# GpSimd subtractions for T2 and T4 of the weights' differences in a decoder layer's gate and up projections

## The chip, the cores and the metric

The kernel runs on one core of one Trainium2 chip. The metric is the device time of one execution in microseconds; the time before is the median of three runs. The profile is of one execution of its own.

## What is computed

The reference is one layer of a decoder (16 meta tokens ahead of 512 positions, width 1024): sparse attention, a layer norm, a SwiGLU feed-forward of width 2816, a second layer norm. The change lies in the feed-forward's first half:

```
def swiglu(h, w_gate, w_up, w_down):
    return (jax.nn.silu(h @ w_gate) * (h @ w_up)) @ w_down

ffn = swiglu(h, ffn_w_gate[i], ffn_w_up[i], ffn_w_down[i])
h = layer_norm(DEEPNORM_ALPHA * h + ffn, ln2_g[i], ln2_b[i])
```

## The kernel before

Every matmul works on a value split in two (a rounded high part, which ScalarE copies, and the rest, which a subtraction gives), so that three products of parts (high·high, high·low, low·high) stand for one fp32 product. Engines run in the order in which the program lists their instructions.

The gate and up projections go through 22 blocks f of 128 features of each. A block's weights are a 2 by 2 matrix of pieces, each 128 partitions by 512 columns: c0 = gate, first half of the depth; c1 = up, first half; c2 = up, second half; c3 = gate, second half. They lie side by side in `wgu[f]`. Blocks 1 to 21 use the Strassen-Winograd scheme: seven products of 12 matmuls instead of eight. Four of them take differences of weights:

- T1 = c1 − c0 (the program's product number 5), T3 = c2 − c1 (number 7),
- T2 = c2 − T1 (number 6), T4 = c3 − T2 (number 4).

Numbers 1, 2 and 3 take c0, c3 and c2 as they are. From block 3 on the products run in the order (f,5), (f,6), (f,2), (f,7), (f+1,1), (f,3), (f,4); `order` holds the list of all of them, and step n of the loop at the end of `trunk` issues product n.

Before product n a step does, in this order: `after` evaluates product n−1 (VectorE adds it to others: m after 6, v and uu after 7, uu after 3, sg and hid after 4; ScalarE's silu after 2 and 4; VectorE's m must have read the bank before product 7 adds to it, and uu before product 3 does); `prepare` splits the weights of the product four steps on (`right_part`: ScalarE writes the high part w, VectorE the low part w); `begin` starts the loads and the differences of later blocks, by distances in steps from (f,5), which `base[f]` holds:

```
LEAD = 4
LOAD_X, SUM_A, LOAD_Y, SUM_B, SUM_C = 20, 13, 11, 7, 3
```

`load_x` and `load_y` load c0,c1 (tile r_x, "upper") and c2,c3 (tile ry, "lower") by SyncE's queue. `sums_a` makes T1 and T3 at once: ScalarE writes −(c0,c1) into a wide tile T (128 by 1024), and a DMA on GpSimd's queue reads c1,c2 from memory and adds them to it (`plus`, line 899). `sums_b` makes T2: ScalarE writes −T1 into a third piece of the wide tile, and an accumulating DMA adds c2. `sums_c` makes T4 the same way from T2, in a tile of its own, with c3. There are two wide tiles, so that T of block f+2 takes the place of block f's. GpSimd does nothing else in this stage from block 3 on.

Of the kernel before, what the change touches and what calls it, by code (L numbers as in the profile page):

```python
# [14 lines left out]
ALU = mybir.AluOpType  # L15
# [58 lines left out]


LEAD = 4
LOAD_X, SUM_A, LOAD_Y, SUM_B, SUM_C = 20, 13, 11, 7, 3
TAIL = 4


# [40 lines left out]
def trunk(ctx, tc, a, out):  # L121
    nc = tc.nc
# [8 lines left out]
    def unit(name, dt=F32, tag="u"):  # L131
        return up.tile([P, UNIT], dt, name=name, tag=tag, bufs=UNITS[tag])
# [25 lines left out]
    def act_copy(o, i, scale=1.0):  # L158
        nc.scalar.activation(o, i, AF.Copy, scale=scale)  # L159
# [680 lines left out]
    upper, lower = {}, {}  # L840
# [54 lines left out]
    right, tsum = {}, {}  # L895

    def plus(o, f, c0, c1):

        nc.gpsimd.dma_start(o, a["wgu"][f][:, c0:c1], accum_op=ALU.add)  # L899
# [7 lines left out]

    def sums_b(f):

        act_copy(tsum[f, 6], tsum[f, 5], scale=-1.0)  # L910
        plus(tsum[f, 6], f, 1024, 1536)

    def sums_c(f):

        tsum[f, 4] = unit(f"T4{f}", tag="kq")[:, :512]
        act_copy(tsum[f, 4], tsum[f, 6], scale=-1.0)
        plus(tsum[f, 4], f, 1536, 2048)

    def begin(n):

        for f in range(2, NF):
            if n == base[f] - LOAD_X and f > 2:
                load_x(f)
            if n == base[f] - LOAD_Y:
                load_y(f)

            if f > 2 and n == max(base[f] - SUM_A, order.index((f - 2, 7)) - LEAD + 2):
                sums_a(f)
            if n == base[f] - SUM_B:
                sums_b(f)  # L930
            if n == base[f] - SUM_C:
                sums_c(f)
# [292 lines left out]
    for b in range(NB):  # L1225
        if b:
            po[1, b] = bank(f"po1{b}", "mm")
        if b == 1:
            normed(0)
            sums_a(1)  # L1230
        if b == 2:

            nc.scalar.activation(small("silu", 1, bufs=6), half_neg, AF.Silu)
        if b == 3:
            sums_b(1)
            prepare(6)
        for k in range(0 if b else 6, KT):
            out_terms(1, k, b)
            if b > 1 and k == LATE:
                turn_norm(b - 2)  # L1240
                normed(b - 1)
        residual(1, b)
        norm(b)
    for n, x in enumerate(order):
        if n == 1:
            sums_a(2)
            normed(3)
        if n == 3:
            turn_norm(2)
            sums_c(1)  # L1250
        if n:
            after(*order[n - 1])
        if n == 5:
            turn_norm(3)
            left_sum(5)
        prepare(min(n + LEAD, len(order)))
        begin(n)
        if n in (7, 9, 12):
            left_sum({7: 6, 9: 7, 12: 3}[n])
        product(*x)  # L1260
        if n == len(order) - 8:
            load(g_ff, 0)
            load(g_ff, 1)
        if n == len(order) - 4:
            hidden_parts(4)
        if n == len(order) - 2:
            cut(g_ff, 0)
# [134 lines left out]
```

## Time and profile before

| | |
|---|---|
| median of 3 runs | 679.12 us (678.54 to 680.46) |
| the profiled execution's own time | 681.46 us |
| its span, first to last instruction | 679.7 us |
| TensorE busy, share of the span | 654.9 us, 96% |
| VectorE / ScalarE / GpSimd busy | 507.9 / 390.5 / 243.2 us |
| DMA queue of GpSimd (q0) | 22.55 MB, 19.8% of 16 engines' span |

The stages along the span: projections and attention up to about 313 us, gate and up projections from 313 to 550 us, the down projection and the last norm to the end. PE stands for TensorE's matmuls, PEld for its weight loads, DVE for VectorE, ACT for ScalarE, POOL for GpSimd. A tile's name (T, w, ry) covers all its buffers; so T in a row can be T1, T2, T3 or T4. L159 and L162 are the helpers `act_copy` and `sub`, L1177 the helper `add` of `after`, so that only tiles tell what such a row is.

### The profile page before, as it was taken

The page shows a single profiled execution, that of the slowest core. Times are in us where ns is not written, and L with a number is a line of the kernel's source. Part 1 is how long each engine was busy: PE and PEld are TensorE (multiplying, and loading weights), DVE is VectorE, ACT ScalarE, POOL GpSimd, SP SyncE. Part 2 cuts the span into 40 slices and gives each one's busy share as a digit, 9 for nine tenths or more (in the row PEclk, how much of TensorE's full clock was granted, in tenths as well). Part 3 has the DMA queues.
Part 4 walks back from the last instruction along what each step waited for, and adds up shares of the span by engine and source line. Part 5 has one row for each costly group of instructions (what it writes and reads, how often), then busy time and mean ns, then how long its engine had stood idle before and what let it go on. Part 6 is the DMA issues. An engine that isn't in the chain of part 4 may idle for free.

```text
span 679.7 us, 11626 instructions
## 1 busy us (share of the span) xinstructions
PE 654.9 (96%) x4196; PEld 588.7 (87%) x4196; DVE 507.9 (75%) x1064; ACT 390.5 (57%) x775; POOL 243.2 (36%) x286
## 2 busy tenths in 40 slices
PE   8999999999999999999899999999999999999995
PEld 6888787888998897889799999899999988888884
DVE  5589898888987888777876767667676676687536
ACT  5573512467777675736766767657666556535420
POOL 2063812497776676556222223222222100011003
PEclk9999999999999999999999999999999999999998
DMA  6547130542242336535688998898997757755611
GB/s 237 174 146 261 60 76 7 148 151 76 71 118 71 111 79 213 158 102 132 138 187 193 205 223 177 199 204 190 225 199 158 203 185 241 234 168 192 203 47 62
DMA packets 41177, 105.80 MB, mean 156 GB/s; under 512 B 4784, under 2 KB 9952, under 8 KB 41120
## 3 DMA queue, kind: packets, MB, share of 16 engines
q1 hardware_dynamic: 31328, 82.12, 37.6%
q0 software_dynamic: 9360, 22.55, 19.8%
q8 instruction: 33, 0.54, 0.3%
q10 hardware_dynamic: 432, 0.39, 0.2%
q14 instruction: 24, 0.20, 0.1%
HBM read 96.88 MB, written 5.27 MB: 150 GB/s over the span
## 4 chain that ended last, share of the span: by engine, by line
PE 38%; issue 33%; DMA 12%; DVE 7%; ACT 5%; POOL 4%; SPq 0%; DVEq 0%; POOLq 0%; ACTq 0%
DMA T<-in_wgu 11%; PE po L773 6%; PE av L728 3%; POOL T L899 3%; PE pv L290 2%; PE pv L288 2%; PE pv L289 2%; PE pt L698 2%; ACT T L159 2%; PE p_q L290 2%; PE p_q L289 2%; PE p_q L288 2%; PE p_k L288 1%; PE p_k L290 1%; PE p_k L289 1%
## 5 line engine op out<-in xcount | busy, mean ns | idle before, releaser
L899 POOL DMA_DIRECT2D T<-in_wgu x63 | 54.7, 869 | 163.2 <-ACT T L159 152.9
L1319 PE MATMUL pd<-h_wd,hp 128*128 128x512 f32 (+1 forms) x324 | 91.1, 366 | 0.0
L162 DVE TENSOR_TENSOR w<-T,w 128x512 fp32r<-128x512 f32 x84 | 57.7, 688 | 24.7 <-ACT w L159 24.0
L1152 PE MATMUL pb<-s,w 128*128 128x256 f32 x504 | 68.2, 285 | 4.5 <-DVE m L1177 2.9
L1152 PE MATMUL pd<-s,w 128*128 128x256 f32 x504 | 67.4, 284 | 2.4 <-DVE uu L1177 1.7
L1152 PE MATMUL pa<-s,w 128*128 128x256 f32 x504 | 67.5, 284 | 1.8 <-ACT m L159 1.8
L1152 PEld LDWEIGHTS pb<-s,w 128*128 128x128 f32 x504 | 63.4, 192 | 6.1 <-ACT T L159 3.8
L1319 PEld LDWEIGHTS pd<-h_wd,hp 128*128 128x128 f32 x324 | 58.6, 189 | 10.1
L1152 PEld LDWEIGHTS pd<-s,w 128*128 128x128 f32 x504 | 63.2, 192 | 3.4 <-ACT T L159 2.3
L1152 PEld LDWEIGHTS pa<-s,w 128*128 128x128 f32 x504 | 63.5, 192 | 2.0 <-ACT m L159 2.0
L162 DVE TENSOR_TENSOR l_wd<-r_wd,h_wd 128x1024 fp32r<-128x1024 f32 x36 | 44.0, 1224 | 28.1 <-ACT h_wd L159 27.9
L672 POOL TENSOR_TENSOR lg<-lg,rec 128x144 f32<-128x144 f32 (+1 forms) x64 | 52.5, 844 | 22.7 <-DVE rec L670 21.9
L1319 PE MATMUL pd<-l_wd,hp 128*128 128x512 f32 (+1 forms) x162 | 59.7, 368 | 0.1
L159 ACT ACTIVATE h_wd<-r_wd 128x1024 fp32r<-128x1024 f32 x36 | 38.0, 1058 | 34.2 <-PE pd L1319 17.7
L159 ACT ACTIVATE w<-T 128x512 fp32r<-128x512 f32 x84 | 50.4, 621 | 5.8 <-DMA T<-in_wgu 5.6
L646 POOL TENSOR_TENSOR bm<-score,tz 128x256 f32<-128x256 f32 (+1 forms) x64 | 43.7, 714 | 16.0 <-DVE mn L655 15.5
L1040 POOL TENSOR_TENSOR fr<-fr,half_neg 128x1 f32<-128x1 f32 x4 | 4.0, 1006 | 121.8 <-DVE fr L1039 121.3
L663 ACT ACTIVATE lg<-lg,mn 128x272 f32<-128x272 f32 (+1 forms) x64 | 36.3, 570 | 11.6 <-DVE mn L655 11.6
L288 PE MATMUL p_k<-hTh,h_wk 128*128 128x264 f32 x128 | 37.8, 295 | 2.3 <-DVE q L331 2.3
L159 ACT ACTIVATE T<-T 128x512 f32<-128x512 f32 x42 | 26.4, 630 | 18.3 <-DMA T<-in_wgu 18.1
L290 PE MATMUL p_k<-hTh,l_wk 128*128 128x264 f32 x128 | 36.5, 285 | 0.0
L289 PE MATMUL p_k<-hTl,h_wk 128*128 128x264 f32 x128 | 36.4, 284 | 0.0
(360 smaller groups left out, 1739.4 us busy)
## 6 DMA issues: line engine op xcount, KB each, us to landing
r_wd<-in_wd SPq DMA_DIRECT2D x36, 512.0 KB, 4.2
r_x<-in_wgu SPq DMA_DIRECT2D x22, 512.0 KB, 8.7
T<-in_wgu POOLq DMA_DIRECT2D x21, 512.0 KB, 7.7
T<-in_wgu POOLq DMA_DIRECT2D x42, 256.0 KB, 5.3
ry<-in_wgu SPq DMA_DIRECT2D x20, 512.0 KB, 6.9
kb<-ka SPq DMA_DIRECT2D x32, 132.0 KB, 2.3
r_wq<-in_wq SPq DMA_DIRECT2D x8, 512.0 KB, 4.5
r_wk<-in_wk SPq DMA_DIRECT2D x8, 512.0 KB, 3.4
```

The source lines that it names most:

```text
L159: nc.scalar.activation(o, i, AF.Copy, scale=scale)
L162: eng.tensor_tensor(out=o, in0=x, in1=y.bitcast(F32), op=ALU.subtract)
L288: nc.tensor.matmul(o, lh, rh, start=i == 0, stop=False)
L289: nc.tensor.matmul(o, lh, rl, start=False, stop=False)
L290: nc.tensor.matmul(o, ll, rh, start=False, stop=i == KT - 1)
L646: nc.gpsimd.tensor_tensor(out=bm.at(b, W[b] - n, W[b]), in0=mask.at(b, W[b] - n, W[b]), in1=tzs[h][:, 256 - n :], op=ALU.add)
L663: nc.scalar.activation(lg.blk(b), lg.blk(b), AF.Exp, bias=mn[:, i : i + 1], scale=-1.0, accum_out=den[:, b : b + 1])
L672: nc.gpsimd.tensor_tensor(out=lg.blk(b), in0=lg.blk(b), in1=rec[:, b : b + 1].to_broadcast([P, W[b]]), op=ALU.mult)
L773: nc.tensor.matmul(po[hf, b], l[:, bs], r, start=k == 0 and i == 0, stop=k == KT - 1 and i == 2)
L899: nc.gpsimd.dma_start(o, a["wgu"][f][:, c0:c1], accum_op=ALU.add)
L1152: nc.tensor.matmul(o, l[:, ks], r[:, k], start=first and k + j == 0, stop=last and k == 3 and j == 2, skip_group_check=not (first and last),)
L1319: nc.tensor.matmul(pd[o], l[:, bs], r[:, c0:c1], start=f == 0 and i == 0, stop=f == NF - 1 and i == 2)
```

## The change

For blocks 2 to 21, T2 and T4 are each one subtraction by GpSimd from the tile ry that was loaded for the products 2 and 3, and from T1 or T2. ScalarE's negations and the accumulating DMAs of these two are gone there. The two steps are issued two products later than before. Block 1, and T1 and T3 of all blocks, stay as they are.

```
-LOAD_X, SUM_A, LOAD_Y, SUM_B, SUM_C = 20, 13, 11, 7, 3
+LOAD_X, SUM_A, LOAD_Y, SUM_B, SUM_C = 20, 13, 11, 5, 1
...
     def sums_b(f):
 
+        if f > 1:
+            nc.gpsimd.tensor_tensor(out=tsum[f, 6], in0=lower[f][:, :512], in1=tsum[f, 5], op=ALU.subtract)
+            return
         act_copy(tsum[f, 6], tsum[f, 5], scale=-1.0)
         plus(tsum[f, 6], f, 1024, 1536)
 
     def sums_c(f):
 
         tsum[f, 4] = unit(f"T4{f}", tag="kq")[:, :512]
+        if f > 1:
+            nc.gpsimd.tensor_tensor(out=tsum[f, 4], in0=lower[f][:, 512:], in1=tsum[f, 6], op=ALU.subtract)
+            return
         act_copy(tsum[f, 4], tsum[f, 6], scale=-1.0)
         plus(tsum[f, 4], f, 1536, 2048)
```

GpSimd's queue in the middle of the stage, two blocks of the kernel before. In each group of three the first row is T1 and T3 of a block (128 by 1024), the second T4 of the block ahead of it, the third T2 of the block of the first row; the names in brackets are what the instruction waits for (DMASW is a DMA of GpSimd's queue, DMAHW one of SyncE's).

```order
260 L899 DMA T_5873<-in_wgu 128x1024 [waits DMASW5_49,DMASW3_49,Activation_49]
261 L899 DMA T_5932<-in_wgu 128x512 [waits DMASW4_49,Activation_49]
262 L899 DMA T_5873<-in_wgu 128x512 [waits Activation_49]
263 L899 DMA T_6007<-in_wgu 128x1024 [waits DMASW6_49,DMASW0_49,Activation_49]
264 L899 DMA T_6066<-in_wgu 128x512 [waits DMASW7_49,Activation_49]
265 L899 DMA T_6007<-in_wgu 128x512 [waits Activation_49]
```

The same place in the changed kernel, two blocks: T1 and T3 of a block, then T2 and T4 of the block ahead of it.

```order
247 L899 DMA T_5315<-in_wgu 128x1024 [waits Activation_49]
248 L911 TENSOR_TENSOR T_5183<-ry,T_5183 128x512 [waits DMAHW7_49,DMASW7_49]
249 L920 TENSOR_TENSOR T_5409<-ry,T_5183 128x512 [waits Pool_49]
250 L899 DMA T_5447<-in_wgu 128x1024 [waits Activation_49]
251 L911 TENSOR_TENSOR T_5315<-ry,T_5315 128x512 [waits DMAHW1_49,DMASW0_49]
252 L920 TENSOR_TENSOR T_5541<-ry,T_5315 128x512 [waits Pool_49]
```

So both subtractions of block f+1 stand right behind the DMA that makes T1 and T3 of block f+2, with nothing between them, and T4's waits only for T2's.

ScalarE's order over one block of the changed kernel (T_5051 is the wide tile of block f+1, T_5145 T4 of block f; T_4919 the wide tile of block f, T_5183 that of f+2). Its first row is for (f,7), the second for (f+1,1).

```order
455 L159 ACTIVATE w_7_5164<-T_4919 128x512
456 L159 ACTIVATE w_1_5180<-r_x_4922 128x512
457 L159 ACTIVATE T_5183<-r_x_5054 128x1024
458 L159 ACTIVATE w_3_5202<-ry 128x512
459 L1197 ACTIVATE sg_5218<-pa_5111 128x256
460 L159 ACTIVATE w_4_5220<-T_5145 128x512
461 L159 ACTIVATE w_5_5240<-T_5051 128x512
462 L159 ACTIVATE m_5256<-pa_5243 128x256
463 L159 ACTIVATE w_6_5258<-T_5051 128x512
464 L159 ACTIVATE w_2_5274<-ry 128x512
465 L1206 ACTIVATE sg_5218<-sg_5218 128x256
```

The kernel before has the same rows and two more: the negation for T2 of a block between its first and second row, and the one for T4 between the rows of w_5 and m. The orders of VectorE, TensorE and SyncE are the same in both kernels.

## Rows read from the trace of the kernel before

**Rows 1.** The page: busy us and share of the span, by engine.

```profile
PE 654.9 (96%) x4196; PEld 588.7 (87%) x4196; DVE 507.9 (75%) x1064; ACT 390.5 (57%) x775; POOL 243.2 (36%) x286
```

**Rows 2.** Timeline, PE: (3,6) and (21,6). Start us, us, engine line operation.

```profile
353.67 1.60 PE L1152 MATMUL pb<-s,w 128*128 128x256 f32 x12
...
543.12 1.60 PE L1152 MATMUL pb<-s,w 128*128 128x256 f32 x12
```

**Rows 3.** Waits from 352.2 to 541.7 us: total us, times, longest.

```profile
ACT sg L1200 <- DVE sg L1177: 34.5, 17, 2.7
...
ACT T L159 <- DMA T<-in_wgu: 16.4, 28, 1.9
```

**Rows 4.** Timeline, a block in which TensorE waited: 428 to 431 us.

```profile
428.64 0.63 ACT L159 ACTIVATE T<-T 128x512 f32<-128x512 f32 x1 [1.95 <-DMA T<-in_wgu]
...
430.43 0.42 DVE L1177 TENSOR_TENSOR m<-pb,m 128x256 f32<-128x256 f32 x1
...
430.99 1.67 PE L1152 MATMUL pb<-s,w 128*128 128x256 f32 x12 [1.42 <-DVE m L1177]
```

**Rows 5.** Timeline, a block without a wait of TensorE: 478.5 to 485.8 us.

```profile
478.55 1.60 PE L1152 MATMUL pd<-s,w 128*128 128x256 f32 x12
...
480.27 0.68 DVE L162 TENSOR_TENSOR w<-T,w 128x512 fp32r<-128x512 f32 x1
...
481.37 1.05 ACT L159 ACTIVATE T<-r_x 128x1024 f32<-128x1024 f32 x1
...
482.32 0.61 ACT L159 ACTIVATE w<-ry 128x512 fp32r<-128x512 f32 x1
482.71 0.86 POOL L899 DMA_DIRECT2D T<-in_wgu  x1 [0.61 <-ACT T L159]
...
482.97 0.69 DVE L162 TENSOR_TENSOR w<-ry,w 128x512 fp32r<-128x512 f32 x1 [0.44 <-ACT w L159]
...
484.00 0.69 DVE L162 TENSOR_TENSOR w<-T,w 128x512 fp32r<-128x512 f32 x1 [0.34 <-ACT w L159]
...
484.61 0.42 DVE L1177 TENSOR_TENSOR v<-pb,m 128x256 f32<-128x256 f32 x1
485.07 0.42 DVE L1177 TENSOR_TENSOR uu<-pd,v 128x256 f32<-128x256 f32 x1
...
485.75 1.60 PE L1152 MATMUL pd<-s,w 128*128 128x256 f32 x12
```

**Rows 6.** Groups by form, POOL: a 128x512 subtraction alone. Busy us, mean ns.

```profile
L162 POOL TENSOR_TENSOR w<-r_x,w 128x512 fp32r<-128x512 f32 x2 | 2.6, 1289 | 3.1 <-ACT w L159 3.1
```

**Rows 7.** Timeline of the attention, DVE and POOL: 274.7 to 278.8 us.

```profile
274.77 1.88 POOL L672 TENSOR_TENSOR lg<-lg,rec 128x400 f32<-128x400 f32 x2
...
275.63 1.57 DVE L162 TENSOR_TENSOR atl<-att,ath 128x512 fp32r<-128x512 f32 x1
276.61 1.46 POOL L162 TENSOR_TENSOR l_wo<-r_wo,h_wo 128x384 fp32r<-128x384 f32 x1
277.12 1.63 DVE L162 TENSOR_TENSOR l_wo<-r_wo,h_wo 128x640 fp32r<-128x640 f32 x1
```

**Rows 8.** Instructions of tile atl, of line L162 on POOL: ns min/median/max.

```profile
L162 DVE TENSOR_TENSOR atl<-att,ath x8: 693/1409/1601, 167.1 to 288.4; 128x512 fp32r<-128x512 f32 x8
...
L162 POOL TENSOR_TENSOR l_wo<-r_wo,h_wo x4: 1006/1010/1462, 241.4 to 276.6; 128x384 fp32r<-128x384 f32 x4
```

**Rows 9.** Timeline of the stage's start: 335.7 to 338.9 us.

```profile
335.71 0.87 POOL L899 DMA_DIRECT2D T<-in_wgu  x1 [1.35 <-ACT T L159]
...
336.58 1.29 DVE L1124 TENSOR_TENSOR q<-q,S 128x512 f32<-128x512 f32 x2
337.30 1.23 ACT L159 ACTIVATE s<-q 128x512 fp32r<-128x512 f32 x2 [1.36 <-DVE q L1124]
...
338.85 1.69 PE L1152 MATMUL pa<-s,w 128*128 128x256 f32 x12 [1.78 <-ACT m L159]
```

**Rows 10.** DMA issues: KB each, median us to landing.

```profile
T<-in_wgu POOLq DMA_DIRECT2D x21, 512.0 KB, 7.7
...
ry<-in_wgu SPq DMA_DIRECT2D x20, 512.0 KB, 6.9
```

## The prediction

> **What bounds the kernel now.** I read the page first: TensorE is busy for 654.9 us, 96% of the span [rows 1], so only its pauses, and what makes it pause, can change the time. The stage that the change touches is the gate and up projections. In a block without a pause five products take 485.75 − 478.55 = 7.20 us [rows 5], 1.44 us each, so a block of seven takes 10.08 us at least. From (3,6) to (21,6) are 18 blocks: 543.12 − 353.67 = 189.45 us [rows 2], against 18 × 10.08 = 181.44. **TensorE loses 8.0 us there**, 0.44 us a block.
>
> What it loses them to is in the waits: ScalarE's negations sat 28 times, 16.4 us in all, until a DMA of T had landed [rows 3]. A block shows how such a wait gets to TensorE [rows 4]: the negation for T2 stood 1.95 us for T1's landing, everything behind it on ScalarE came late, with that the low part for (f+1,1) on VectorE, behind that the addition m, and TensorE, which may not start product 7 before m, stood 1.42 us. T4 hurts in the same way through the split of its tile. These DMAs land after 7.7 us at the median [rows 10].
>
> **The change part by part.**
>
> *Removed: 40 negations and 40 accumulating DMAs.* With the negations no instruction of ScalarE waits for T1 to land except T1's own split, and that comes a block later. T4 and T2 land no more at all. I take all 8.0 us of the 18 blocks as gone: **−8.0**. ScalarE's time for the negations itself is worth nothing: it idles 34.5 us in this stretch only for the addition sg ahead of a silu [rows 3], and that comes from TensorE.
>
> *Added: 40 subtractions on GpSimd.* One of this form takes 1.29 us [rows 6] and GpSimd is nearly idle, so its own time would cost nothing. The price is what it does to VectorE. The rows show it [rows 7]: atl, a subtraction of two tiles in SBUF, began at 275.63 while GpSimd multiplied until 276.65, and took 1.57 us, to 277.20; alone it takes 0.69 [rows 8]. So it ended 0.55 us after GpSimd let go: it stood still meanwhile. GpSimd's next, l_wo, began at 276.61 and took 1.46 instead of its 1.01 [rows 8]: it waited for atl. VectorE's next l_wo, 277.12, ended 0.68 us after that one. The two engines take turns, and an instruction that waits has the next turn.
>
> Now a block, in us after the start of (f,5), 478.55 [rows 5]. The low part for product 7 ends at 1.72 + 0.68 = 2.40 on VectorE. It reads the wide tile of block f, which the copy T<-r_x of block f+2 overwrites. That copy started at 2.82 behind the negation; now it starts at about 2.43, which the low part sets. GpSimd's DMA began 1.34 after the copy, so at 3.77, and takes 0.86: T2's subtraction may start at 4.67. Its inputs are there: ry was loaded a block ahead and lands in 6.9 us [rows 10]. The high part of product 3 began 0.95 after the copy and takes 0.61, so its low part runs on VectorE from 4.03 to 4.72, ahead of GpSimd; GpSimd works until **5.96**. The low part for product 4 comes to VectorE at 5.45 (484.00), set by TensorE's product 2 and the silu behind it, so not earlier than now. It stands until 5.96 and ends 0.55 later, at 6.51 instead of 6.14. Behind it are v (0.61 after its start now, so at 6.43) and uu, which ends at 7.30. TensorE started 0.14 us after such an addition where it waited for one (430.85 to 430.99) [rows 4], so product 3 starts at 7.45 instead of 7.20. **A pause of 0.25 us in each of 18 blocks: +4.5.** It is not made up: TensorE has nothing to catch up with, and the rest of a block hangs on it. v and uu themselves read PSUM and one tile in SBUF, and I take it that they stand for nobody. T4's subtraction gets its turn when the low part of 4 is done, at 6.5, and ends at 7.7; the low part of the next T1 then ends at 8.3, and its product starts at 10.3: nothing.
>
> *The stage's start.* In step 12 T2 and T4 of block 2 meet the last combination of the activations. GpSimd is free at 336.58 [rows 9], VectorE's two subtractions q start then; I let VectorE have the first turn, GpSimd the second, so the second q ends about 1.1 late, ScalarE's s and m behind it too, and TensorE, which already stood there for m, stands 1.1 longer: **+1.1**. Bounds: 0, and 2.3 if GpSimd is first. Smaller waits for DMAs further on there go: −0.4.
>
> *The end.* For block 21 no DMA stands ahead on GpSimd, so both subtractions run as soon as ry has landed, early in block 20, where VectorE's low parts and m have less room: **+0.8** (0 to 1.4).
>
> *The moved steps* (5 and 1 in place of 7 and 3) cost nothing: T2's split follows the subtraction by about 1.7 us. The queue of SyncE does not change.
>
> Sum: −8.0 + 4.5 + 1.1 − 0.4 + 0.8 = **−2.0** on the profiled execution's 681.46. On the median, 679.12, that is 677.1. The median lies 2.3 us lower, and the pauses hang on landings, which differ from run to run, so it may hold less to give back: I take **677.5**.
>
> A page's rule speaks against the change. The Trainium skill (GPSIMD Engine Reference, Engine selection) gives elementwise work on a tile to VectorE, since GpSimd is about half as fast with two inputs; the rows agree, 1.29 against 0.69 us. By that rule alone both subtractions would cost 1.2 us a block more than on VectorE; here they cost only what VectorE waits.
>
> **The rivals.**
>
> *All turns fall into gaps* (672.5). If T2's subtraction ends before 5.45, or VectorE stands less than these attention rows say, nothing is left of the 4.5: −6.5. For it: the overlap is only 0.5 us. Against it: each step of the walk is tied to the copy T<-r_x, and that to the low part of 7.
>
> *Later by half a microsecond* (685). If T2's subtraction ends at 6.4 (GpSimd slow to start behind its DMA, or VectorE's turn ahead of it longer), the pause is 0.7 a block, 12.6 us: −8.0 + 12.6 + 1.5 = +6. It decides from a pause of 0.36 a block, a subtraction that ends at 6.07: close. For it: two turns of another engine stretched l_wo by 0.45 [rows 8].
>
> *Both subtractions ahead of a low part* (697). If T2's gets its turn before the low part of 3, that one waits for it and the low part of 4 for T4's: 1.4 us a block, 25 in all. Against it: the low part of 3 would have to come 0.64 later against GpSimd, and both follow the same copy. The Trainium skill (SBUF — State Buffer, SBUF: two separate sides) states such a lock: whoever starts first keeps the shared ports for the whole instruction. By it T4's turn too would block in full whatever meets it.
>
> *The pauses stay* (about 682). The change takes these DMAs away, but T1 and T3 still come by DMA, and T2 on GpSimd now also waits for ry. If landings were still late, the pauses would stay beside the new ones. Against it: ry and T1 have ten microseconds, and a block moves 1.5 MB instead of 2.0.
>
> **How the numbers follow.** 0.3% is 2.0 us, about what a measurement of this kernel can tell from no change. Forecast (674.5 to 681) 0.50, of which 0.20 faster, 0.27 no change, 0.03 slower; gaps 0.20, faster; half a microsecond later 0.18, slower; both ahead 0.05, slower; pauses stay 0.07, of which 0.05 no change and 0.02 slower. So faster 0.40, no change 0.32, slower 0.28. The range leaves out the 697 and the tails: 671 to 687.
>
> **What would show it.** Right: no wait of ScalarE for T, except a few; low parts of 4 that take about 1.1 us while a subtraction of GpSimd runs; PE's pauses at product 3, 0.25 each, behind uu; 18 blocks in 186 us. Wrong: the low part of 4 at 0.69 (gaps), or pauses at 7 behind m (both ahead), or ScalarE still waiting for DMAs.

## The result, and the profile after

The changed kernel takes **734.46 us** (median of 3 runs, 734.34 to 743.59) against 679.12: a ratio of **1.0849, interval 1.0788 to 1.0910**. 677.5 was forecast, with 671 to 687 as the range: slower by far, and outside. The profiled execution took 743.59 us, the longest of the three, with a span of 741.8 us; the sums below are made against it and the 679.7 us of before.

The page of the changed kernel, first its busy row, its clock row and two groups of instructions ("busy, mean ns" and behind the second bar the idle time before):

```profile
PE 685.3 (92%) x4196; PEld 616.8 (83%) x4196; DVE 560.1 (75%) x1064; ACT 368.2 (50%) x735; POOL 268.0 (36%) x286
...
PEclk9999999999999999998989899898898899999998
...
L162 DVE TENSOR_TENSOR w<-T,w 128x512 fp32r<-128x512 f32 x84 | 76.6, 931 | 4.6 <-ACT w L159 4.5
...
L162 DVE TENSOR_TENSOR w<-ry,w 128x512 fp32r<-128x512 f32 x40 | 58.6, 1464 | 11.9 <-ACT w L159 11.9
```

Against [rows 1], TensorE is busy 30 us longer with the same 4196 matmuls, so some of them were slower; VectorE is busy 52 us longer with the same 1064 instructions. A low part of either group took 0.68 to 0.69 us before [rows 5]; now the means are 0.93 and 1.46. And the clock row, in tenths of the full clock, has eights in the second half, where most of the gate and up projections lie.

The waits from 313 to 620 us (total us, times, longest):

```profile
ACT sg L1206 <- DVE sg L1183: 103.6, 21, 5.8
...
PE pd L1158 <- DVE uu L1183: 33.0, 18, 2.2
...
PE pa L1158 <- ACT m L159: 4.6, 1, 4.6
```

The waits of ScalarE for a T to land [rows 3] are gone. In their place TensorE stands for uu ahead of product 3, in 17 of the 18 blocks some 2 us each, and once 4.6 us for m at the stage's start.

(3,6) and (21,6), the rows that answer to [rows 2]:

```profile
359.25 1.00 PE L1158 MATMUL pb<-s,w 128*128 128x256 f32 x7
...
602.52 0.64 PE L1158 MATMUL pb<-s,w 128*128 128x256 f32 x4
```

| stretch | before, us | after, us | difference |
|---|---|---|---|
| to (3,6) | 353.67 | 359.25 | +5.6 |
| (3,6) to (21,6), 18 blocks | 189.45 | 243.27 | +53.8 |
| (21,6) to the end of the span | 136.58 | 139.28 | +2.7 |

One block, which answers to [rows 5]; (f,5) starts at 481.49, and the last rows are product 3 of the block and the two products behind it. "The low part of 3" is short for VectorE's subtraction that makes the low part w for product 3 (w<-ry at 485.59 here), "the low part of 4" for the one of product 4 (w<-T at 488.03).

```profile
481.49 1.60 PE L1158 MATMUL pd<-s,w 128*128 128x256 f32 x12
...
483.98 1.06 ACT L159 ACTIVATE T<-r_x 128x1024 f32<-128x1024 f32 x1 [0.37 <-issue]
...
485.33 0.88 POOL L899 DMA_DIRECT2D T<-in_wgu  x1 [9.77 <-ACT T L159]
485.59 2.51 DVE L162 TENSOR_TENSOR w<-ry,w 128x512 fp32r<-128x512 f32 x1 [0.60 <-ACT w L159]
...
485.95 1.60 POOL L911 TENSOR_TENSOR T<-ry,T 128x512 f32<-128x512 f32 x1
...
487.62 1.62 POOL L920 TENSOR_TENSOR T<-ry,T 128x512 f32<-128x512 f32 x1
488.03 1.77 DVE L162 TENSOR_TENSOR w<-T,w 128x512 fp32r<-128x512 f32 x1
...
489.73 0.41 DVE L1183 TENSOR_TENSOR v<-pb,m 128x256 f32<-128x256 f32 x1
490.17 0.42 DVE L1183 TENSOR_TENSOR uu<-pd,v 128x256 f32<-128x256 f32 x1
...
490.74 2.52 PE L1158 MATMUL pd<-s,w 128*128 128x256 f32 x12 [1.89 <-DVE uu L1183]
...
493.06 2.29 PE L1158 MATMUL pe<-s,w 128*128 128x256 f32 x12
...
495.19 1.00 PE L1158 MATMUL pd<-s,w 128*128 128x256 f32 x7
```

The low part for product 3 began 0.26 us after the DMA, as it did before [rows 5], and 0.36 us *ahead* of the start recorded for T2's subtraction. Yet it stood until that one ended (485.95 + 1.60 = 487.55) and was done 0.55 later, at 488.10. Then GpSimd had the next turn with T4, until 489.24, and the low part for product 4 stood until then: again 0.56 to its end. Behind it came v and uu, and product 3 started 9.25 us into the block instead of 7.20: **a pause of 2.05 us**. (Its row names 1.89 us of idle time: a row gives 12 matmuls 1.60 us, while the next product can start 1.44 us after them. Pauses are here counted by starts.)

The two products behind the pause took 490.74 to 495.19, 4.45 us instead of 2 × 1.44: **1.57 us more**. The windows around the pause of the block ahead tell why (window, its length, busy time and instructions of PE, PEld, DVE, ACT, POOL, then the granted clock, the DMA share and GB/s):

```profile
474.95:477.05 2.10, 0.21 (x2) 0.03 (x2) 2.07 (x4) 1.42 (x3) 0.62 (x1) 1.00 1.04 271
477.05:481.45 4.40, 4.40 (x24) 4.40 (x25) 2.08 (x4) 0.00 (x0) 0.00 (x0) 0.61 0.45 177
481.45:488.70 7.25, 7.25 (x62) 7.20 (x60) 5.85 (x7) 4.46 (x8) 3.29 (x3) 1.00 0.27 41
```

In the pause the clock reads 1.00, over the 24 matmuls after it 0.61, then 1.00 again: a part of the 24 ran at 1.2 GHz instead of 2.4. One matmul takes 1.44 / 12 = 0.12 us at the full clock and so 0.12 more at half of it; by that, 1.57 us are some 13 of the 24 (an estimate). A block is 10.08 + 2.05 + 1.57 = 13.70 us, and the timeline has 13.7 in 15 of the 17 (13.89 and 13.97 in the others). The last of the 18 blocks takes 10.08: there no DMA stands ahead of the subtractions. So −8.0 + 17 × 3.62 = +53.5, measured +53.8.

### The profile page after: what moved, and what is told of

Its sections match the earlier page's. It is cut to its first block, busy times and chain, and to the rows that moved or that the text cites. A ratio compares the mean times of both kernels' runs of the same rounds, so it can differ in the third digit from the quotient of the medians.

```text
span 741.8 us, 11545 instructions
## 1 busy us (share of the span) xinstructions
PE 685.3 (92%) x4196; PEld 616.8 (83%) x4196; DVE 560.1 (75%) x1064; ACT 368.2 (50%) x735; POOL 268.0 (36%) x286
## 4 chain that ended last, share of the span: by engine, by line
issue 22%; DVE 12%; PE 10%; ACT 6%; POOL 1%; DVEq 0%; POOLq 0%
DVE w L162 7%; PE pd L1158 6%; PE pe L1158 5%; ACT T L159 2%; ACT w L159 2%; DVE hid L1211 1%; DVE uu L1183 1%; DVE sg L1183 1%; ACT sg L1206 1%; DVE v L1183 1%; POOL fr L1046 1%; DVE su L1335 0%; DVE y L1067 0%; DVE y L1334 0%; POOL T L920 0%
## 5 line engine op out<-in xcount | busy, mean ns | idle before, releaser
L1158 PE MATMUL pd<-s,w 128*128 128x256 f32 x504 | 81.6, 322 | 33.0 <-DVE uu L1183 33.0
L1158 PEld LDWEIGHTS pd<-s,w 128*128 128x128 f32 x504 | 75.3, 226 | 36.1 <-ACT w L159 35.7
L899 POOL DMA_DIRECT2D T<-in_wgu x23 | 20.5, 890 | 184.0 <-ACT T L159 173.9
L162 DVE TENSOR_TENSOR w<-T,w 128x512 fp32r<-128x512 f32 x84 | 76.6, 931 | 4.6 <-ACT w L159 4.5
L162 DVE TENSOR_TENSOR w<-ry,w 128x512 fp32r<-128x512 f32 x40 | 58.6, 1464 | 11.9 <-ACT w L159 11.9
L162 DVE TENSOR_TENSOR l_wd<-r_wd,h_wd 128x1024 fp32r<-128x1024 f32 x36 | 44.0, 1224 | 30.6 <-ACT h_wd L159 30.3
L1206 ACT ACTIVATE sg<-sg 128x256 f32<-128x256 f32 x21 | 8.8, 418 | 103.6 <-DVE sg L1183 103.6
L159 ACT ACTIVATE h_wd<-r_wd 128x1024 fp32r<-128x1024 f32 x36 | 38.0, 1057 | 36.6 <-DMA r_wd<-in_wd 17.6
L1158 PE MATMUL pe<-s,w 128*128 128x256 f32 x252 | 47.7, 360 | 0.0
L1158 PEld LDWEIGHTS pe<-s,w 128*128 128x128 f32 x252 | 47.3, 280 | 0.0
```

The costliest lines, as they stand in the source:

```text
L162: eng.tensor_tensor(out=o, in0=x, in1=y.bitcast(F32), op=ALU.subtract)
L1158: nc.tensor.matmul(o, l[:, ks], r[:, k], start=first and k + j == 0, stop=last and k == 3 and j == 2, skip_group_check=not (first and last),)
L1206: nc.scalar.activation(ev[f, "g"][:, hi], ev[f, "g"][:, hi], AF.Silu)
```

## The experiments

The theory: a subtraction of GpSimd whose waits are met takes its turn while the DMA ahead of it is still being issued, before its own recorded start, so a low part that begins just behind the DMA loses. Rivals: the issuing of the DMA alone holds VectorE; the moved steps (5 and 1) do the harm; GpSimd's subtractions cost this wherever they stand. All edits are shown against the changed kernel, with calls cut short by three dots. The blocks are (3,6) to (21,6) of each trace, worked out as in [rows 2]; a ratio is to the kernel before, on the same chip.

| kernel | us, median (range) | ratio (interval) | 18 blocks, us |
|---|---|---|---|
| e1_gap | 734.98 (731.98–736.77) | 1.0772 (1.0727–1.0818) | 237.59 |
| e2_ahead | 686.19 (684.14–688.80) | 1.0065 (1.0036–1.0093) | 190.44 |
| e3_none | 674.78 (673.42–676.18) | 0.9892 (0.9849–0.9935) | 181.44 |
| e4_vector | 676.14 (675.02–678.63) | 0.9926 (0.9900–0.9952) | 181.93 |
| e5_unmoved | 698.91 (697.87–700.99) | 1.0261 (1.0194–1.0328) | 201.62 |
| e6_wait | 690.14 (688.26–691.65) | 1.0127 (1.0071–1.0184) | 193.22 |
| e7_t2only | 687.19 (686.88–689.39) | 1.0088 (1.0063–1.0113) | 192.59 |
| e8_t4only | 679.86 (677.19–682.06) | 0.9974 (0.9943–1.0006) | 185.09 |
| e9_best | 674.73 (674.13–676.52) | 0.9909 (0.9881–0.9937) | 182.03 |
| e10_late | 675.10 (673.41–676.83) | 0.9908 (0.9877–0.9940) | 182.09 |

**e1_gap: a small GpSimd instruction between the DMA and T2's subtraction.**

```
         if f > 1:
+            nc.gpsimd.memset(gap, 0.0)
             nc.gpsimd.tensor_tensor(out=tsum[f, 6], ...)
```

> One small memset (128x1) on GpSimd between the DMA for T1/T3 and T2's subtraction. Theory claim (a subtraction that stands directly behind a DMA in GpSimd's queue claims the port it shares with VectorE while that DMA is still being issued, so it goes ahead of the low part of product 3, which began earlier): the low part of 3 takes 0.69 us again instead of 2.5, TensorE's pause before product 3 shrinks from 2.0 to about 0.25 us, its clock does not fall, time 677 us (674 to 682). Rival DMA (issuing the DMA itself keeps VectorE's two-input instructions out): the low part of 3 still ends only after T2's subtraction, time 730 to 736.

A miss: nothing is gained. Two rows of the first of the 18 blocks, then those of another block:

```profile
359.31 0.88 POOL L900 DMA_DIRECT2D T<-in_wgu  x1 [7.08 <-ACT T L159]
359.56 0.69 DVE L162 TENSOR_TENSOR w<-ry,w 128x512 fp32r<-128x512 f32 x1 [0.76 <-ACT w L159]
...
490.58 0.89 POOL L900 DMA_DIRECT2D T<-in_wgu  x1 [9.77 <-ACT T L159]
490.83 2.55 DVE L162 TENSOR_TENSOR w<-ry,w 128x512 fp32r<-128x512 f32 x1 [0.59 <-ACT w L159]
...
491.16 0.41 POOL L912 MEMSET gap<- 128x1 f32 x1
491.23 1.60 POOL L913 TENSOR_TENSOR T<-ry,T 128x512 f32<-128x512 f32 x1
```

The low part is held as before, to 0.55 after the subtraction's end, although the memset stands between. So it is in 16 of the 17 blocks that have such a DMA. What claims the turn early is thus not tied to the subtraction being next; this run doesn't tell the theory from the DMA alone. The first block is an exception: the low part began 0.25 us behind the DMA as in the others, memset and subtraction followed (359.89 and 359.96), T1 and ry had landed by 357.6 (7.3 us after 350.01, 6.8 after 350.75), and yet it took 0.69. Being next behind the DMA with its waits met is thus not the whole condition; what differed there is open. The run also told something of the clock, below.

**e2_ahead: both subtractions ahead of the DMA.**

```
-LOAD_X, SUM_A, LOAD_Y, SUM_B, SUM_C = 20, 13, 11, 5, 1
+LOAD_X, SUM_A, LOAD_Y, SUM_B, SUM_C = 20, 13, 11, 7, 7
```

> Both subtractions of a block are issued seven products ahead (7 and 7 instead of 5 and 1), so that they stand ahead of the next DMA in GpSimd's queue and run as soon as ry has landed. Theory claim: they meet only low parts that have two microseconds of room; no pause at product 3, no fall of the clock, time 671 to 676 us. Rival DMA: the low part of 3 falls into the issue of the DMA and is held for some 0.6 us, time 678 to 690. If GpSimd's turns harm VectorE wherever they fall: over 690.

48 us better than the change, but above what was expected, a miss: with no DMA ahead, T2's subtraction now starts when T1 lands (92.3 us of waits for it in 14 blocks), which falls beside the low parts of 3 and 4. Most blocks cost 0.3 to 0.4 us of pause. The time lies in the range that was given to the rival of the DMA, but not by its mechanism: the DMA stands behind both subtractions, away from the low part of 3. In the block with the longest pause it was T2's subtraction that held it, begun 0.03 us earlier:

```profile
454.19 1.29 POOL L911 TENSOR_TENSOR T<-ry,T 128x512 f32<-128x512 f32 x1 [7.69 <-DMA T<-in_wgu]
454.22 1.81 DVE L162 TENSOR_TENSOR w<-ry,w 128x512 fp32r<-128x512 f32 x1 [0.60 <-ACT w L159]
```

**e3_none: T2 and T4 left out** for blocks 2 to 21 (products 6 and 4 take c2 and c3 as they are), so no negation, no DMA and no subtraction for them.

```
-            nc.gpsimd.tensor_tensor(out=tsum[f, 6], in0=lower[f][:, :512], ...)
+            tsum[f, 6] = lower[f][:, :512]
...
-            nc.gpsimd.tensor_tensor(out=tsum[f, 4], in0=lower[f][:, 512:], ...)
+            tsum[f, 4] = lower[f][:, 512:]
```

> Leaves out T2 and T4 of blocks 2 to 21: the products 6 and 4 take c2 and c3 themselves; neither negation nor DMA nor subtraction stands there. It bounds what the removed DMAs were worth. If TensorE's 8.0 us of pauses all came from them: 671 us. If another wait takes their place: 675 to 679. The clock at 1.00 through the stage in both cases.

All 18 blocks take 10.08 us: 181.44, the −8.0 of the prediction to the digit. That is what there was to be gained. The whole time gains 6.7; in the profiled execution the start and the end took 0.3 and 1.2 us longer.

**e4_vector: the same subtractions on VectorE**, in the same steps.

```
-            nc.gpsimd.tensor_tensor(out=tsum[f, 6], ...)
+            nc.vector.tensor_tensor(out=tsum[f, 6], ...)
...
-            nc.gpsimd.tensor_tensor(out=tsum[f, 4], ...)
+            nc.vector.tensor_tensor(out=tsum[f, 4], ...)
```

> The same subtractions, in the same steps, on VectorE instead of GpSimd. Theory claim: nothing is shared any more, each takes 0.69 us, T2's lies between the low parts of 3 and 4 where 0.6 us are free, T4's behind the low part of 2; time 672 to 677 us. Rival load (VectorE simply has no room for two more instructions a block, and the loss of the changed kernel is the load, not the turns): 685 us or more.

It beats both kernels, the one before by 0.7%. The timeline of a block, whose (f,5) starts at 474.77 and the next block's at 484.85:

```profile
478.75 0.86 POOL L899 DMA_DIRECT2D T<-in_wgu  x1 [9.21 <-ACT T L159]
479.01 0.69 DVE L162 TENSOR_TENSOR w<-ry,w 128x512 fp32r<-128x512 f32 x1 [0.71 <-ACT w L159]
...
479.62 0.68 DVE L911 TENSOR_TENSOR T<-ry,T 128x512 f32<-128x512 f32 x1
...
484.65 0.68 DVE L920 TENSOR_TENSOR T<-ry,T 128x512 f32<-128x512 f32 x1
```

The same subtraction takes 0.68 us instead of GpSimd's 1.29 [rows 6], and VectorE's own order puts it behind the low part of 3. 17 of the 18 blocks take 10.08. The run also speaks against the DMA alone: the low part of 3 begins 0.26 us behind the same DMA and takes its 0.69.

**e5_unmoved: the steps as before the change** (7 and 3), the subtractions on GpSimd.

```
-LOAD_X, SUM_A, LOAD_Y, SUM_B, SUM_C = 20, 13, 11, 5, 1
+LOAD_X, SUM_A, LOAD_Y, SUM_B, SUM_C = 20, 13, 11, 7, 3
```

> The subtractions in the steps of the kernel before (7 and 3): T2's stands ahead of the next DMA and waits for T1 and ry to land, T4's stands directly behind that DMA. Theory claim (on GpSimd an instruction whose waits are met takes its turn for the shared port while the instruction ahead of it is still running, a DMA's issue included): one subtraction only goes ahead of the low part of 3; pause before product 3 about 0.85 us a block, clock does not fall, time 690 us (684 to 697). Rival: it is T2's subtraction alone, or the load of GpSimd as such, that does it: below 682, or over 720.

Now T4's subtraction alone stands behind the DMA, and it holds the low part of 3 in the same way; the low part of 4 (487.78, 0.68) is free. Seventeen blocks take 11.09 to 11.72 us, so the pauses are 1.0 to 1.6 us, at a clock of 1.00. That is above what was expected (0.85 us a block, 684 to 697 us in all): in a block of 11.63 T2's subtraction, which waited for ry, held another instruction of VectorE as well (hid at 470.71, 1.23 us instead of 0.69), and the start keeps 4.6 us (358.28 against 353.67).

```profile
485.08 0.89 POOL L899 DMA_DIRECT2D T<-in_wgu  x1 [2.87 <-ACT T L159]
485.33 2.52 DVE L162 TENSOR_TENSOR w<-ry,w 128x512 fp32r<-128x512 f32 x1 [0.59 <-ACT w L159]
...
485.69 1.61 POOL L920 TENSOR_TENSOR T<-ry,T 128x512 f32<-128x512 f32 x1
```

So the moved steps decide which subtraction stands there, and it is the place behind the DMA that does the harm.

**e6_wait: T2's subtraction made to wait for the low part of 3** (GpSimd first copies one column of it).

```
         if f > 1:
+            if f > 3:
+                nc.gpsimd.tensor_copy(gap, right[f - 1, 3][1][:, :1].bitcast(F32))
             nc.gpsimd.tensor_tensor(out=tsum[f, 6], ...)
```

> The changed kernel with a copy of one column by GpSimd ahead of T2's subtraction that reads the low part of product 3 of the block before, so that GpSimd cannot take its turn ahead of that low part. Theory claim: the low part of 3 takes 0.69 us again, T2's subtraction runs behind it, the low part of 4 stands until its end; pause before product 3 of 0.3 to 0.6 us a block, no fall of the clock, time 680 to 688 us. Rival (the issue of the DMA keeps VectorE's two-input instructions out, whatever follows): the low part of 3 is still held for 0.6 us or more and the time stays over 700.

```profile
479.18 0.88 POOL L900 DMA_DIRECT2D T<-in_wgu  x1 [6.59 <-ACT T L159]
479.44 0.69 DVE L162 TENSOR_TENSOR w<-ry,w 128x512 fp32r<-128x512 f32 x1 [0.59 <-ACT w L159]
...
480.20 0.18 POOL L913 COPY gap<-w 128x1 f32<-128x1 f32 x1
480.34 1.29 POOL L914 TENSOR_TENSOR T<-ry,T 128x512 f32<-128x512 f32 x1
480.86 1.32 DVE L162 TENSOR_TENSOR w<-T,w 128x512 fp32r<-128x512 f32 x1 [0.73 <-ACT w L159]
```

This decides against the DMA alone, as e4 does: it is the same DMA, and the low part begins the same 0.26 us behind it, but takes 0.69 instead of 2.51. What differs is that the instruction behind the DMA has a wait that isn't met; that it is a small one doesn't do it, as e1 shows. From here on the block goes as the prediction's walk had it: the low part of 4 stands for T2's subtraction (480.34 + 1.29 = 481.63) and ends 0.55 later; the pause is 0.64 us, since the subtraction begins later than in the walk. A little above the 680 to 688 expected; the start, which block 2 and 3 set without the wait, keeps 4.3 us (358.02 against 353.67).

**e7_t2only and e8_t4only: one subtraction on GpSimd**, the other as in the kernel before, in its old step. The edit of e7 stands here; e8's has steps 7 and 1, and takes the three lines out of `sums_b` instead.

```
-LOAD_X, SUM_A, LOAD_Y, SUM_B, SUM_C = 20, 13, 11, 5, 1
+LOAD_X, SUM_A, LOAD_Y, SUM_B, SUM_C = 20, 13, 11, 5, 3
...
         tsum[f, 4] = unit(f"T4{f}", tag="kq")[:, :512]
-        if f > 1:
-            nc.gpsimd.tensor_tensor(out=tsum[f, 4], ...)
-            return
```

> T2 by GpSimd as in the changed kernel (step 5), T4 by negation and DMA as before (step 3). Theory claim: T2's subtraction goes ahead of the low part of 3, but no second turn follows, so the pause before product 3 is about 0.9 us a block instead of 2.0 and the clock stays; some pauses on T4's DMA come back: 688 to 700 us. If the loss of the clock needs no long pause: over 710.

> T4 by GpSimd (step 1), T2 by negation and DMA as before (step 7). T4's subtraction stands behind a DMA but waits for T2's DMA to land, some 5 us after its issue. Theory claim: a turn is taken only when the waits are met, so it falls behind uu, where VectorE has room: no pause before product 3, 675 to 682 us. If any subtraction behind a DMA harms the low part of 3, waits met or not: 690 or more.

e7 is no confirmation: its time, 687.19, lies just under the expected range, and the low part of 3 was not held. But it narrows the moment of the claim:

```profile
477.79 0.86 POOL L899 DMA_DIRECT2D T<-in_wgu  x1 [6.65 <-ACT w L159]
477.79 0.69 DVE L162 TENSOR_TENSOR w<-ry,w 128x512 fp32r<-128x512 f32 x1 [0.54 <-ACT w L159]
...
478.35 1.64 POOL L911 TENSOR_TENSOR T<-ry,T 128x512 f32<-128x512 f32 x1
```

A low part that begins *with* the DMA won in every block; one that begins 0.26 later lost in all of the change. The low part of 4 then stands (1.35 us), and a block has 0.6 of pause. In e8 T4's subtraction waits for T2 to land by DMA; that falls beside uu or behind it, and 11 of the 18 blocks take 10.10 to 10.14: as expected. Six others lose 0.4 to 1.0 us, and there TensorE stands for m (1.9 us in 6 waits), as in [rows 4], since T2 still comes by DMA.

**e9_best and e10_late: two versions that should cost nothing.** In both, block 2 is left as in the kernel before, in its old steps. e9 has VectorE's subtractions (the edit of e4) from block 3 on. e10 has GpSimd's; T2's is issued one product later, and waits, by the copy of e6, for the low part of product 4 instead of 3:

```
-LOAD_X, SUM_A, LOAD_Y, SUM_B, SUM_C = 20, 13, 11, 5, 1
+LOAD_X, SUM_A, LOAD_Y, SUM_B, SUM_C = 20, 13, 11, 4, 1
...
+            nc.gpsimd.tensor_copy(gap, right[order[base[f] - 1]][1][:, :1].bitcast(F32))
             nc.gpsimd.tensor_tensor(out=tsum[f, 6], in0=lower[f][:, :512], ...)
```

> Both subtractions on VectorE from block 3 on; block 2's T2 and T4 as in the kernel before (negation and accumulating DMA, steps 7 and 3). If the 2.1 us that e4_vector lost between (1,6) and (2,6) came from block 2's two subtractions on VectorE, this interval goes back to about 14 us and the time is about 674 (673 to 676); if they came from elsewhere, 676.

> GpSimd's two subtractions as in the change, but T2's is made to wait for the low part of product 4 of the block ahead (a copy of one column that reads it, step 4), and block 2 is left as in the kernel before. If the whole cost of the change is that a subtraction takes its turn ahead of a low part on which product 3 hangs, nothing is left of it: GpSimd works from about 6.2 to 8.8 us of a block, where VectorE has v and uu, which read PSUM, and the low part of 5, which has 2 us of room. Blocks of 10.08 and 672 to 677 us. If GpSimd's subtractions cost something wherever they stand (v and uu held too, or the low part of 5 late for product 5), pauses of 0.5 us or more stay and the time is 682 or more.

e10 answers the last rival. A block of it:

```profile
479.80 0.69 DVE L162 TENSOR_TENSOR w<-T,w 128x512 fp32r<-128x512 f32 x1 [0.23 <-ACT w L159]
...
480.56 0.18 POOL L912 COPY gap<-w 128x1 f32<-128x1 f32 x1 [1.05 <-DVE w L162]
480.70 1.30 POOL L913 TENSOR_TENSOR T<-ry,T 128x512 f32<-128x512 f32 x1
480.86 0.42 DVE L1185 TENSOR_TENSOR uu<-pd,v 128x256 f32<-128x256 f32 x1
...
481.47 1.64 PE L1160 MATMUL pd<-s,w 128*128 128x256 f32 x12
```

GpSimd subtracts while VectorE's uu, which reads PSUM, runs beside it in its usual 0.42 us; the low parts behind it are held, but have room. Sixteen of the 18 blocks take 10.10 to 10.12 us: 0.03 lost instead of 3.62, from the same subtractions on the same engine. e9's blocks take 10.08 from the second of the 18 on. Both versions beat the kernel before, by 0.9%; between them and e4 the intervals overlap. What e9 was to show of block 2 missed: (1,6) to (2,6) went to 15.47 us, not to about 14 as before (13.96). TensorE's pause for m is back at 1.78 us, as in [rows 9], but the clock behind it read 0.79 from 338 to 346 us, where the kernel before read 1.00.

## Why the prediction was wrong

**What failed** is one step: "so its low part runs on VectorE from 4.03 to 4.72, ahead of GpSimd; GpSimd works until 5.96". I ordered the two by the time at which each could begin, and let the subtraction begin when the DMA had been issued. The walk up to there was right within 0.07 us (copy 2.49, DMA 3.84, low part 4.10 in the block above), and the turn went to the other engine. GpSimd's recorded work fits the walk too: the subtraction's row begins 0.26 us before the DMA's ends (485.33 + 0.88 = 486.21), and counted back from its end by the 1.29 us of [rows 6] it begins at 486.26, when a low part of 0.69 us from 485.59 would have been all but done. So the turn was taken before that work began. That a subtraction which stands behind a DMA and could go ahead claims early is shown by the change against e4 and e6 (the same low part at the same distance from the DMA) and fits e5 and e7, and e1 but for its first block. Where in time the claim lies is only bounded, by an estimate: after the DMA's start, and not later than 0.4 us behind it (the low part had 0.55 of its 0.69 us still to do when it was let go, so it was stopped within 0.14 us of its start at 0.26). Why it is so early is open, and so is what spared the one block of e1. A second term was put at nothing and was not: the moved steps. With the old ones (e5) the 18 blocks take 201.62 us instead of 243.27, since the new ones put T2's subtraction behind the DMA as well.

**The rival that came true** was "both subtractions ahead of a low part", at 0.05. Its mechanism was right, its condition was not: no 0.64 us were needed. Its price, 1.4 us a block, was too small: 2.05 of pause, and 1.57 of clock that no case had. Its sign was wrong too: the pauses stand at product 3 behind uu (33.0 us, 18 times), not at 7 behind m. The Trainium skill (SBUF — State Buffer, SBUF: two separate sides) lets whoever starts first keep the shared ports for the whole instruction. The trace agrees in the price (each held instruction ended 0.55 us after the other's end); but who started first can't be read from the recorded starts, by which VectorE was first by 0.36 us.

**The clock** was in no case. A pause of 2.05 us was followed by the slower matmuls in all 17 blocks (13.67 to 13.97 us each); pauses of 0.6 to 1.6 us in e5 and e6 were not. But e1 has two blocks with a full pause and no fall (12.23 and 12.24 us), beside its 13.70, and why is open:

```profile
393.40:407.10 13.70, 11.79 (x86) 11.61 (x85) 9.95 (x14) 5.88 (x12) 3.86 (x4) 0.88 0.46 116
407.10:419.34 12.24, 10.31 (x87) 10.14 (x86) 9.98 (x14) 5.89 (x12) 3.87 (x4) 1.00 0.47 129
```

Of the 3.62 us a block the pause is 2.05 and the clock, where it fell, 1.57. Whether fewer falls make the 9 us by which the other two runs are shorter than the profiled one was not tried; their mean clocks, 0.960 and 0.957 against 0.953, point that way.

**What held.** The −8.0: e3 has it exactly, and e4, e9 and e10 have 7.4 to 7.5 of it with the subtractions in. In the changed kernel it was outweighed by what the turns and the clock cost. The 0.55 us after the release, and v and uu standing for nobody. That the pauses on landings would not stay: no wait of ScalarE for T is left, and the DMAs land after 5.4 us (T) instead of 7.7 [rows 10].

**What was mis-sized.** The 18 blocks, −8.0 + 4.5 in the sum, came to +53.8. The start, +1.1 with a bound of 2.3, came to +5.6. By the same claim T2's and T4's subtractions of block 2 both ran before the two q:

```profile
335.62 0.87 POOL L899 DMA_DIRECT2D T<-in_wgu  x1 [8.72 <-ACT T L159]
335.87 2.47 DVE L162 TENSOR_TENSOR w<-T,w 128x512 fp32r<-128x512 f32 x1 [0.71 <-ACT w L159]
336.18 1.61 POOL L911 TENSOR_TENSOR T<-ry,T 128x512 f32<-128x512 f32 x1
337.86 1.60 POOL L920 TENSOR_TENSOR T<-ry,T 128x512 f32<-128x512 f32 x1
338.27 2.35 DVE L1130 TENSOR_TENSOR q<-q,S 128x512 f32<-128x512 f32 x2
...
341.60 2.93 PE L1158 MATMUL pa<-s,w 128*128 128x256 f32 x12 [4.62 <-ACT m L159]
```

TensorE stood 4.62 us for m instead of 1.78 [rows 9], and the slower matmuls behind it make the other 2.7; the −0.4 for smaller waits didn't show ((2,6) to (3,6) took 9.07 us, 8.97 before). The end (+0.8) came to nothing: the last of the 18 blocks, with no DMA ahead, takes 10.08. Behind (21,6) the changed kernel took 2.7 us more, where the change issues nothing. For 1.9 us of it TensorE stood there for the split of the down projection's weights, where the kernel before didn't stand; ScalarE had waited 17.6 us in all for their loads, 12.9 before. Why those came later stays open.

## What to carry to other kernels

Two engines that lock each other out don't go by the times at which you think each is ready: an instruction that stands with its waits met behind a DMA on its queue can already hold the turn. So where such work moves to another engine, give it a wait on the instruction that must go first, and choose that so that what runs beside it reads PSUM or has room: here this, with block 2 left as it was and T2 one product later, took 734.5 us to 675.1 (1.085 of the kernel before to 0.991). And price a new pause of TensorE of some 2 us with the clock behind it, not by its length only.

## What the runs showed of the hardware that was not expected

- A low part on VectorE, recorded as begun 0.36 us before GpSimd's subtraction, was held by it for its whole time (2.51 us instead of 0.69). With an unmet wait between DMA and subtraction it was not (e6, 0.69), and where it began with the DMA it was not (e7, 0.69).
- The row of T2's subtraction behind the DMA overlaps the DMA's by 0.26 us and is 0.31 us longer than one alone (1.60 against 1.29).
- The accumulating DMA took GpSimd 0.86 to 0.89 us to issue, and alone it didn't hold the low part that began 0.26 us behind it (e4, 0.69).
- A small memset between the DMA and the subtraction did not let VectorE in (e1, 2.55 us), except in one block of 17 (0.69).
- The granted clock fell to 0.61 over the 24 matmuls after a pause of some 2 us, but kept 1.00 after two such pauses in e1; at the stage's start it read 0.79 from 338 to 346 us in e3, e9 and e10 after the same 1.78 us of standing behind which the kernel before and e8 kept 1.00.
